# Two transformer blocks on one core: feed-forward input products from quarters, and the transposes of normed rows moved one block later

## The chip, the cores and the metric

The program runs on one core of a Trainium2 chip. The metric is the device time of one execution in microseconds (us). TensorE (PE) does the matrix products into PSUM; VectorE (DVE), ScalarE (ACT) and GpSimd (POOL) do the rest; SyncE (SP) issues the transfers.

## The reference, cut to what matters

Two blocks of a network follow one another on rows of width 1024: 512 rows of x and 256 of a context, all in 32-bit floats. There are four feed-forward parts (FFN 1 to 4 here, in order of time), each

```python
def swiglu(h, w_in, w_out):                     # h: T x 1024, w_in: 1024 x 5632, w_out: 2816 x 1024
    gate, up = jnp.split(h @ w_in, 2, axis=-1)
    return (jax.nn.silu(gate) * up) @ w_out
```

FFN 1 and FFN 3 work on T = 768 rows, FFN 2 and FFN 4 on T = 512. Between them lie mixers (linear attention, windowed and differential attention, a state-space scan). Before each FFN a residual sum is normed and scaled by a modulation: `x = layer_norm(ALPHA * x + g * mix(...))`, then `x * (1 + sc) + sh`.

## The kernel before

Every wide product is made of three passes: both factors are split into a high part (a cast, on ScalarE, L57) and a low part (a subtraction, on VectorE, L58), and PE sums high*high, high*low and low*high. `Core.split` does it, for 128x1024 tiles of weights too (`weight`, tiles `raw`, `whi`, `wlo`; three buffers of `raw`, four each of `whi` and `wlo`).

`ffn` (L363) has two stages. The input stage runs over j = 0 to 21. For each j it loads 128 gate columns and 128 up columns of `w_in` (each 128 x 8 x 128), splits them, and `mm_a` (L82) multiplies 8 pieces of the inner dimension in three passes: 48 matmuls of 512 columns, and for T = 768 another 48 of 256. `leave` takes silu (L385, ACT) and the product (L386, DVE) and stores the tile to DRAM (`gd`). It also runs `nfill` pieces of other work (`run_fill`): the products with `w_ada` and `mod_w` of later modulations, done on DVE (L223) for one or two vectors. The first two j are led in by `lead`: pieces of 256 rows, so that PE can work on the rows that are normed first while the last rows are still under way.

The output stage (L410 on) runs over the two halves of the rows, and for each over the 22 j in 18 groups: it loads 128 rows of `w_out` and the piece of `gd`, splits both, and `mm_b` (L96, L106) adds to the PSUM tiles of the half's rows, 128 rows at a time. In the last group each 128 rows go through `end.tail`: gate, residual, norm, and `to_hT` (L257): eight PE transposes (L269), scale and shift (L277 ACT, L280 DVE), and the split into `hhi` and `hlo`, the factors of the next stage. `rows_out` (L343) does the same for a mixer's output product.

The Tile framework fixes the order of each engine's queue ahead of the run from readiness and a priority that follows the program's order; `high_priority` moves weight loads and splits 400 places forward. A queue, SP's too, runs in order: an instruction that waits holds up those behind it.

Of the kernel before, what the change touches and what calls it, by code (L numbers as in the profile page):

```python
# [16 lines left out]
P = 128  # L17
D = 1024
# [6 lines left out]
class Core:  # L25


    def __init__(self, ctx, tc):
# [12 lines left out]
        self.fill = []  # L41

# [214 lines left out]
    def to_hT(self, pool, src, t, h, sc=None, bi=None, act=2):  # L257
# [3 lines left out]
        nc = self.nc  # L261
        hhi, hlo = h
# [80 lines left out]
def rows_out(c, w, parts, j0, T, put, px=False, scale=None):  # L343

    ws = [c.wrows(w, (j0 + i) * P, scale=scale) for i in range(len(parts))]
    ops = [(gh, gl, wh[:, 0], wl[:, 0]) for (gh, gl), (wh, wl) in zip(parts, ws)]
    for t in range(T // P):
        if px and t % 3 == 2:
            ps = [c.ps("px"), c.ps("px")]
            c.mm_b(ops, t * P, [(ps[0], 0, 512), (ps[1], 512, 512)])  # L350
            put(t, ps)
        else:
            pb = c.big()
            c.mm_b(ops, t * P, [(pb[:, :512], 0, 512), (pb[:, 512:], 512, 512)])
            put(t, [pb])

# [6 lines left out]
def ffn(c, h, T, w_in, w_out, end, nfill=2, lead=(0, 256)):  # L363
# [5 lines left out]
    nx = 512  # L369
    gd = [c.dram.tile([P, T], F32, name=c.nm("gd")) for _ in range(NJ)]  # L370
    with c.tc.tile_pool(name=c.nm("ffn"), bufs=2) as pool:

        def enter(j):
            pb = c.big()
            pc = c.ps("px") if T > nx else None
            og, ou = [(pb[:, :512], 0, nx)], [(pb[:, 512:], 0, nx)]
            if pc is not None:
                og.append((pc[:, :256], nx, 256))
                ou.append((pc[:, 256:], nx, 256))
            return c.wcols(w_in, j * P), c.wcols(w_in, FFN_H + j * P), og, ou  # L380

        def leave(j, og, ou):
            g = pool.tile([P, T], F32, tag="g", name=c.nm("g"), bufs=3)
            for (pg, t0, n), (pu, _, _) in zip(og, ou):
                nc.scalar.activation(g[:, t0 : t0 + n], pg, AF.Silu)  # L385
                nc.vector.tensor_tensor(g[:, t0 : t0 + n], pu, g[:, t0 : t0 + n], ALU.mult)  # L386
            nc.sync.dma_start(gd[j], g)
            if j >= 2:
                c.run_fill(nfill)

        ahead = [enter(j) for j in range(2)]
        for t0 in lead:
            for wg, wu, og, ou in ahead:
                for w_, outs in ((wg, og), (wu, ou)):
                    o, o0, _ = outs[t0 // nx]
                    c.mm_a(w_, h, [(o[:, t0 - o0 : t0 - o0 + 256], t0, 256)])
        for j in range(NJ):
            if j < len(ahead):
                leave(j, *ahead[j][2:])
                continue  # L400
            wg, wu, og, ou = enter(j)
            c.mm_a(wg, h, og)
            c.mm_a(wu, h, ou)
            leave(j, og, ou)
        c.run_fill(999)
        end.gate()
        end.fold()

        half = T // (2 * P)
        for first in (0, half):  # L410
            ts = range(first, first + half)
            c0, n = first * P, half * P
            out = {}

            def load(j):
                wh, wl = c.wrows(w_out, j * P)
                with c.tc.high_priority(offset=WPRIO):
                    gr = pool.tile([P, n], F32, tag="gr", name=c.nm("gr"), bufs=3)
                    nc.sync.dma_start(gr, gd[j][:, c0 : c0 + n])
# [5 lines left out]
            def room(t):  # L425
                if t % 3 == 2:
                    return [c.ps("px"), c.ps("px")]
                return [c.big()]

            js = [range(EDGE)] + [[j] for j in range(EDGE, NJ - EDGE)] + [range(NJ - EDGE, NJ)]  # L430
            for grp in js:
                ops = [load(j) for j in grp]
                for t in ts:
                    if t not in out:
                        out[t] = room(t)
                    c.mm_b(ops, (t - first) * P, halves(out[t]), grp[0] == 0, grp[-1] == NJ - 1)
                    if grp[-1] == NJ - 1:
                        end.tail(t, out[t])
        end.finish()
# [354 lines left out]
class LnTail:  # L794
# [4 lines left out]
    def __init__(self, c, pool, I, l, i, y, gates, resid, sc, xd, keep, hT=None, after=None, out=None, scaled=False):  # L799
        self.c, self.pool, self.y, self.gates = c, pool, y, gates  # L800
        self.resid, self.sc, self.xd, self.keep, self.after, self.out = resid, sc, xd, keep, after, out
        self.T = hT
# [3 lines left out]
        self.rows = (I["ln_g"][l, i : i + 1], I["ln_b"][l, i : i + 1])  # L806

# [36 lines left out]
    def fold(self):  # L844
# [4 lines left out]
        self.h = c.hT(self.T) if self.T else None  # L849

    def tail(self, t, pb):
# [4 lines left out]
        if self.after is None:  # L856
            c.to_hT(self.pool, y, t, self.h, *self.sc["x" if t < 4 else "c"], act=3)
# [21 lines left out]
class AdaTail:  # L879


    def __init__(self, c, pool, y, gates, resid, sc, xd, hT=None, out=None, ahead=2):
        self.c, self.pool, self.y, self.gates = c, pool, y, gates
        self.resid, self.sc, self.xd, self.T, self.out, self.ahead = resid, sc, xd, hT, out, ahead
        self.begun = set()
        self.scale = None

    def gate(self):
        self.g = self.gates()
# [10 lines left out]
    def fold(self):  # L900
        self.sc = self.sc()
        self.h = self.c.hT(self.T) if self.T else None
# [36 lines left out]
def ada_pre(c, pool, x, t, h, sc):  # L939
# [7 lines left out]
    c.to_hT(pool, xr, t, h, *sc, act=3)  # L947


def main(c, I, out, stop=None):  # L950
# [101 lines left out]
    with tc.tile_pool(name="mix0", bufs=1) as mp:  # L1052
# [58 lines left out]
        with tc.tile_pool(name="p1", bufs=1) as pool:  # L1111
            m = [pool.tile([P, KT, 768], F32R, name=f"m1{i}") for i in range(2)]
            for i, x in enumerate((og, od)):
                for t in range(6):
# [3 lines left out]
                        ln_sc("00", 0, 0, "scf0", "shf0", "xc"), xd[0], "xc", 768, out=out if stop == "ln1" else None)  # L1118
# [9 lines left out]
    with tc.tile_pool(name="p2", bufs=1) as pool, tc.tile_pool(name="modp1", bufs=2) as mq:  # L1128
# [4 lines left out]
        y = acc(pool, 6)  # L1133
        ln = LnTail(c, pool, I, 0, 1, y, {v: f"gf0{v}" for v in "xc"}, xdt(0),
                    ln_sc("01", 0, 1, "scm1", "shm1", "xc"), xd[1], "xc" if stop else "x", 768,
                    out=out if stop == "ln2" else None)
        ffn(c, h, 768, I["ffn_w_in"][0], I["ffn_w_out"][0], ln, 3, (0, 256, 512))
# [8 lines left out]
    with tc.tile_pool(name="p3", bufs=1) as pool:  # L1146
# [3 lines left out]
                    scaled=True)  # L1150
# [797 lines left out]
```

## Time and profile before

| what | value |
|---|---|
| median of 3 runs | 3626.3 us (3624.19 to 3632.98) |
| profiled execution, its own time | 3623.33 us |
| its span, first to last instruction | 3621.6 us |
| PE busy | 3479.2 us (96%) |
| DVE busy | 2134.4 us (59%) |
| ACT busy | 1503.7 us (42%) |
| POOL busy | 377.6 us (10%) |
| mean granted TensorE clock | 0.984 |

An engine is busy while one of its instructions runs; matmuls overlap, so a full PE bar means that PE had no idle time, not that it was at its peak. A row of a table of stretches gives the stretch, its length, for PE, PE's weight loads (PEld), DVE, ACT and POOL the busy us and the count of instructions, then the granted clock, the busy share of the DMA engines and GB/s. A row of a timeline gives start, duration, engine, line, operation, tiles, shapes and count; what stands in brackets is the idle time before it and what ended it. A row of waits gives total us, times, longest. A row of instructions of one line gives shortest/median/longest ns.

### The profile page before, as it was taken

The page shows a single profiled execution, that of the slowest core. Times are in us where ns is not written, and L with a number is a line of the kernel's source. Part 1 is how long each engine was busy: PE and PEld are TensorE (multiplying, and loading weights), DVE is VectorE, ACT ScalarE, POOL GpSimd, SP SyncE. Part 2 cuts the span into 40 slices and gives each one's busy share as a digit, 9 for nine tenths or more (in the row PEclk, how much of TensorE's full clock was granted, in tenths as well). Part 3 has the DMA queues.
Part 4 walks back from the last instruction along what each step waited for, and adds up shares of the span by engine and source line. Part 5 has one row for each costly group of instructions (what it writes and reads, how often), then busy time and mean ns, then how long its engine had stood idle before and what let it go on. Part 6 is the DMA issues. An engine that isn't in the chain of part 4 may idle for free. (4 is left out here: it accounts for less than half of the span.)

```text
span 3621.6 us, 48878 instructions
## 1 busy us (share of the span) xinstructions
PE 3479.2 (96%) x18988; PEld 2899.5 (80%) x18988; DVE 2134.4 (59%) x3246; ACT 1503.7 (42%) x2400; POOL 377.6 (10%) x309
## 2 busy tenths in 40 slices
PE   8999989999999999988999999999999999999999
PEld 5877778888878877767877788888887798878887
DVE  7766566554366577766566764443556585663245
ACT  5335533221344455533324632222556464553234
POOL 0001121000010354443000100000000000000000
PEclk9999999999999999989999999999999999999999
DMA  6331125555453233344665754654641112354456
GB/s 231 108 88 30 45 99 178 163 184 169 144 195 107 76 108 99 105 158 159 219 200 181 244 194 132 200 160 140 203 140 46 49 61 73 108 180 151 122 166 218
DMA packets 442652, 509.94 MB, mean 141 GB/s; under 512 B 20808, under 2 KB 355780, under 8 KB 442421
## 3 DMA queue, kind: packets, MB, share of 16 engines
q1 hardware_dynamic: 442421, 506.83, 44.3%
q8 instruction: 149, 2.44, 0.3%
q14 instruction: 82, 0.67, 0.1%
HBM read 446.20 MB, written 56.35 MB: 139 GB/s over the span
## 5 line engine op out<-in xcount | busy, mean ns | idle before, releaser
L58 DVE TENSOR_TENSOR wlo<-raw,whi 128x1024 fp32r<-128x1024 f32 (+1 forms) x524 | 639.9, 1225 | 661.8 <-ACT whi L57 632.9
L57 ACT CAST whi<-raw 128x1024 fp32r<-128x1024 f32 (+1 forms) x524 | 542.4, 1037 | 976.3 <-PE px L92 264.3
L92 PE MATMUL big<-hhi,whi 128*128 128x512 f32 (+1 forms) x2080 | 736.5, 370 | 9.8 <-ACT hhi L57 5.4
L92 PE MATMUL big<-hlo,whi 128*128 128x512 f32 (+1 forms) x2080 | 728.8, 367 | 3.6 <-DVE hlo L58 3.6
L92 PE MATMUL big<-hhi,wlo 128*128 128x512 f32 (+1 forms) x2080 | 731.1, 367 | 0.0
L92 PEld LDWEIGHTS big<-hhi,whi 128*128 128x128 f32 x2080 | 383.5, 191 | 85.3 <-issue 8.3
L92 PEld LDWEIGHTS big<-hlo,whi 128*128 128x128 f32 x2080 | 382.3, 191 | 69.8 <-DVE hlo L58 5.2
L92 PEld LDWEIGHTS big<-hhi,wlo 128*128 128x128 f32 x2080 | 382.3, 191 | 65.5 <-issue 1.9
L126 POOL TENSOR_TENSOR s<-s,mhalf 128x1 f32<-128x1 f32 (+1 forms) x106 | 72.8, 688 | 2656.8 <-DVE s L124 2350.3
L92 PE MATMUL px<-hhi,whi 128*128 128x256 f32 (+1 forms) x992 | 310.2, 316 | 3.6 <-ACT dqk L667 1.6
L92 PE MATMUL px<-hlo,whi 128*128 128x256 f32 (+1 forms) x992 | 309.0, 315 | 0.0
L92 PE MATMUL px<-hhi,wlo 128*128 128x256 f32 (+1 forms) x992 | 308.2, 314 | 0.0
L223 DVE SCALAR_TENSOR_TENSOR acc<-graw,silu_c,acc 128x1024 f32<-128x1024 f32 x168 | 211.7, 1292 | 78.0 <-DMA graw<-in_w_ada_dram 42.2
L106 PE MATMUL px<-whi,hhi 128*128 128x256 f32 (+1 forms) x712 | 213.2, 302 | 0.9 <-DVE wqf L620 0.7
L106 PE MATMUL px<-wlo,hhi 128*128 128x256 f32 (+1 forms) x712 | 211.4, 300 | 0.0
L106 PE MATMUL px<-whi,hlo 128*128 128x256 f32 (+1 forms) x712 | 211.1, 300 | 0.0
L92 PEld LDWEIGHTS px<-hhi,whi 128*128 128x128 f32 x992 | 186.3, 189 | 17.0 <-issue 2.1
L92 PEld LDWEIGHTS px<-hlo,whi 128*128 128x128 f32 x992 | 186.3, 189 | 10.7 <-issue 1.7
L92 PEld LDWEIGHTS px<-hhi,wlo 128*128 128x128 f32 x992 | 186.4, 189 | 10.2 <-issue 1.5
L57 ACT CAST ghi<-gr 128x256 fp32r<-128x256 f32 (+1 forms) x176 | 80.8, 460 | 273.8 <-PE px L106 159.0
L106 PE MATMUL big<-whi,ghi 128*128 128x512 f32 x616 | 191.4, 392 | 0.0
L106 PE MATMUL big<-whi,glo 128*128 128x512 f32 x616 | 191.4, 391 | 0.0
(545 smaller groups left out, 5976.8 us busy)
## 6 DMA issues: line engine op xcount, KB each, us to landing
raw<-in_ffn_w_in_dram SPq DMA_DIRECT2D x176, 512.0 KB
raw<-in_ffn_w_out_dram SPq DMA_DIRECT2D x176, 512.0 KB
graw<-in_mod_w_dram SPq DMA_DIRECT2D x80, 512.0 KB
graw<-in_w_ada_dram SPq DMA_DIRECT2D x72, 512.0 KB
raw<-in_mix_w_in_dram SPq DMA_DIRECT2D x42, 512.0 KB
raw<-in_ssd_w_in_dram SPq DMA_DIRECT2D x41, 512.0 KB
gd<-g SPq DMA_DIRECT2D x44, 384.0 KB
gr<-gd SPq DMA_DIRECT2D x88, 192.0 KB
```

The lines of the kernel that those rows point to most:

```text
L57: self.nc.scalar.copy(hi, src)
L58: self.nc.vector.tensor_tensor(lo, src, hi.bitcast(F32), ALU.subtract)
L92: self.nc.tensor.matmul(out, lhsT=w_[:, k, :], rhs=x_[:, k, t0 : t0 + tn], start=st, stop=sp)
L106: self.nc.tensor.matmul(out, lhsT=h_[:, t0 : t0 + P], rhs=w_[:, n0 : n0 + nn], start=st, stop=sp)
L126: nc.gpsimd.tensor_tensor(out=r, in0=v, in1=self.mhalf[:, :n], op=ALU.pow)
L223: nc.vector.scalar_tensor_tensor(a, raw, v[:, k : k + 1], a, ALU.mult, ALU.add)
```

## The change

The input stage takes a 2x2 partition of each j's product: the weights' blocks are (gate, up) x (inner half 1, 2), the rows' blocks are (inner half 1, 2) x (row half 1, 2). Eight products of quarters become seven in the Strassen-Winograd form, each of four pieces, three passes and n = T/2 columns: 84 matmuls of 384 columns (T = 768) or 256 (T = 512). Four sums of weight blocks per j are made on POOL, four sums of row blocks once per FFN on DVE and POOL (`Quarters.sums`). For these each normed 128 rows are stored to DRAM (`fd`) and read back. Intermediate products stay in PSUM and are copied out where a second result needs them. The weights come through four buffers of their own (`sr`) instead of `raw`. The fill runs 2 or 1 pieces per j and the rest in the output stage, one per group. The output stage has its own pool, opened after the input stage's pool closes, with the rows `y` in it.

`to_hT` of a normed tile is not issued at once but put in `c.later`; `flush` issues it behind the matmuls of the next 128 rows, and that of the last tile at the end.

```diff
+    def flush(self):
+        todo, self.later = self.later, []
+        for f in todo:
+            f()
...
     def to_hT(self, pool, src, t, h, sc=None, bi=None, act=2):
+        if isinstance(h, Quarters):
+            f = pool.tile([P, KT, P], F32, tag="hTf", name=self.nm("hTf"), bufs=h.bufs)
...
+            h.put(t, f)
+            return
...
 def rows_out(c, w, parts, j0, T, put, px=False, scale=None):
...
             c.mm_b(ops, t * P, [(pb[:, :512], 0, 512), (pb[:, 512:], 512, 512)])
+            c.flush()
             put(t, [pb])
+    c.flush()
...
+class Quarters:
+    def __init__(self, c, T, bufs=2):
+        self.c, self.n, self.half, self.bufs = c, T // 2, T // (2 * P), bufs
+        self.hi, self.lo = (x.rearrange("p k t -> p (k t)").rearrange("p (b k n) -> p b k n", b=4, k=4) for x in c.hT(T))
+        self.fd = [c.dram.tile([P, KT, P], F32, name=c.nm("fd")) for _ in range(T // P)]
+    def put(self, t, f):
+        c = self.c
+        c.nc.sync.dma_start(self.fd[t], f)
+        o = t % self.half * P
+        if t < self.half:
+            c.split(f.rearrange("p (b k) n -> p b k n", b=2), self.hi[:, 0:2, :, o : o + P], self.lo[:, 0:2, :, o : o + P])
+        else:
+            c.split(f[:, 4:], self.hi[:, 2, :, o : o + P], self.lo[:, 2, :, o : o + P])
+    def factors(self, pool):
+        c = self.c
+        self.t = [pool.tile([P, 3, 4, self.n], F32R, name=c.nm("tq")) for _ in range(2)]
+        q = lambda i: (self.hi[:, i], self.lo[:, i])
+        t = lambda i: (self.t[0][:, i], self.t[1][:, i])
+        return {1: q(0), 2: q(1), 3: q(2), 5: q(3), 6: t(0), 7: t(1), 4: t(2)}
+    def sums(self, pool, last):
+        c, nc = self.c, self.c.nc
+        for i in [i for i in range(self.half) if i != last] + [last]:
+            f1, f2 = (pool.tile([P, KT, P], F32, tag=f"f{j}", name=c.nm("f"), bufs=2) for j in range(2))
+            nc.sync.dma_start(f1, self.fd[i])
+            nc.sync.dma_start(f2, self.fd[i + self.half])
+            s = pool.tile([P, 4, 4, P], F32, tag="ts", name=c.nm("ts"), bufs=1)
+            nc.vector.tensor_tensor(s[:, 0], f2[:, :4], f1[:, :4], ALU.subtract)
+            nc.gpsimd.tensor_tensor(out=s[:, 2], in0=f2[:, 4:], in1=f2[:, :4], op=ALU.subtract)
+            nc.vector.tensor_tensor(s[:, 1], f2[:, 4:], s[:, 0], ALU.subtract)
+            nc.vector.tensor_tensor(s[:, 3], f1[:, 4:], s[:, 1], ALU.subtract)
+            o = slice(i * P, (i + 1) * P)
+            c.split(s[:, 0], self.hi[:, 3, :, o], self.lo[:, 3, :, o])
+            c.split(s[:, 1:], self.t[0][:, :, :, o], self.t[1][:, :, :, o])
...
+def ffn(c, h, T, w_in, w_out, end, nfill=(2, 1), last=None):
...
+    with c.tc.tile_pool(name=c.nm("fa"), bufs=1) as pool:
+        B = h.factors(pool)
+        def weights(j):
+            r = []
+            with c.tc.high_priority(offset=WPRIO):
+                for c0 in (j * P, FFN_H + j * P):
+                    x = pool.tile([P, KT, P], F32, tag="sr", name=c.nm("sr"), bufs=4)
+                    nc.sync.dma_start(x, w_in[:, c0 : c0 + P].rearrange("(k p) n -> p k n", p=P))
+                    r.append(x)
+                def pair(x):
+                    hi = c.whl.tile([P, KT, P], F32R, tag="hi", name=c.nm("whi"))
+                    lo = c.whl.tile([P, KT, P], F32R, tag="lo", name=c.nm("wlo"))
+                    c.split(x, hi, lo)
+                    return (hi[:, :4], lo[:, :4]), (hi[:, 4:], lo[:, 4:])
+                a11, a12 = pair(r[0])
+                a22 = tuple(pool.tile([P, 4, P], F32R, tag=f"a{i}", name=c.nm("a"), bufs=2) for i in range(2))
+                c.split(r[1][:, 4:], *a22)
+                p, q = r[0][:, :4], r[0][:, 4:]
+                u, v = r[1][:, :4], r[1][:, 4:]
+                for o, x, y, op in ((p, p, u, ALU.subtract), (u, u, v, ALU.add), (v, v, p, ALU.subtract),
+                                    (q, q, v, ALU.subtract)):
+                    nc.gpsimd.tensor_tensor(out=o, in0=x, in1=y, op=op)
+                s1, s2 = pair(r[1])
+                s3, s4 = pair(r[0])
+            return {1: a11, 2: a12, 3: s4, 4: a22, 5: s1, 6: s2, 7: s3}
+        def mul(out, j, i, start=False):
+            (wh, wl), (bh, bl) = W[j][i], B[i]
+            for k in range(4):
+                for w_, b_ in ((wh, bh), (wh, bl), (wl, bh)):
+                    nc.tensor.matmul(out, lhsT=w_[:, k], rhs=b_[:, k], start=start and k == 0 and w_ is wh and b_ is bh,
+                                     stop=k == 3 and w_ is wl, skip_group_check=True)
...
+        def first(j):
+            W[j] = weights(j)
+            X[j] = c.ps("px")[:, :n]
+            mul(X[j], j, 1, True)
+            S[j] = {1: room(pool, "p1")}
+            nc.scalar.copy(S[j][1], X[j])
+        def second(j):
...
+            Y[j], Z[j] = pb[:, :n], pb[:, 512 : 512 + n]
+            mul(Y[j], j, 2, True)
+            g = S[j][11] = room(pool, "c11")
+            nc.vector.tensor_tensor(g, Y[j], S[j][1], ALU.add)
+            nc.scalar.activation(g, g, AF.Silu)
+        for j in range(2):
+            first(j)
+            second(j)
+        with c.tc.tile_pool(name=c.nm("fs"), bufs=1) as fp:
+            h.sums(fp, half - 1 if last is None else last)
+        with c.tc.tile_pool(name=c.nm("fm"), bufs=1) as mp:
...
+            def third(j):
+                mul(Z[j], j, 3)
+                u, g = room(mp, "c12", 1), S[j]["g"]
+                nc.vector.tensor_tensor(u, Z[j], S[j][2], ALU.add)
+                nc.scalar.activation(u, u, AF.Silu)
+                nc.vector.tensor_tensor(g[:, n:], u, S[j][22], ALU.mult)
+                nc.sync.dma_start(gd[j], g)
+                c.run_fill(nfill[0])
+            for j in range(NJ + 1):
+                if j < NJ:
+                    sixth(j)
+                if j:
+                    fourth(j - 1)
+                if j < NJ:
+                    mul(Z[j], j, 5, True)
+                if j:
+                    third(j - 1)
+                if 0 < j < NJ - 1:
+                    first(j + 1)
+                if j < NJ:
+                    seventh(j)
+                if 0 < j < NJ - 1:
+                    second(j + 1)
+    with c.tc.tile_pool(name=c.nm("fb"), bufs=1) as pool:
+        end.open(pool)
...
+                if b == 0 and grp[-1] == NJ - 1:
+                    end.gate()
+                    end.fold()
...
+                    c.flush()
                     if grp[-1] == NJ - 1:
                         end.tail(t, out[t])
+                c.run_fill(nfill[1])
+        c.run_fill(999)
+        c.flush()
...
-    c.to_hT(pool, xr, t, h, *sc, act=3)
+    c.later.append(lambda: c.to_hT(pool, xr, t, h, *sc, act=3))
...
-        ffn(c, h, 768, I["ffn_w_in"][0], I["ffn_w_out"][0], ln, 3, (0, 256, 512))
+        ffn(c, h, 768, I["ffn_w_in"][0], I["ffn_w_out"][0], ln)
...
-        ffn(c, h, 512, I["ffn_w_in"][1], I["ffn_w_out"][1], ln)
+        ffn(c, h, 512, I["ffn_w_in"][1], I["ffn_w_out"][1], ln, (1, 1))
...
-        ffn(c, h, 768, I["ffn1_w_in_2"][0], I["ffn1_w_out_2"][0], ad, 3, (512, 0, 256))
+        ffn(c, h, 768, I["ffn1_w_in_2"][0], I["ffn1_w_out_2"][0], ad, last=0)
```

`sixth`, `fourth` and `seventh` multiply into `X` and hand it on in the same way: ACT copies of `X` (`u2`, `u3`), a DVE sum `c22` of `Z` and `u3`, and a DVE product of `X` with `c11` into `g`.

## Rows read from the trace of the kernel before

**Rows 1.** The page, busy time, share and instructions of each engine.
```profile
PE 3479.2 (96%) x18988; PEld 2899.5 (80%) x18988; DVE 2134.4 (59%) x3246; ACT 1503.7 (42%) x2400; POOL 377.6 (10%) x309
```
**Rows 2.** Stretches: FFN 3 and 4 input, 256-column product, FFN 2 output, FFN 4 start.
```profile
2150.00:2450.00 300.00, 300.00 (x1703) 258.29 (x1702) 142.77 (x152) 65.53 (x94) 0.00 (x0) 1.00 0.52 165
3300.00:3500.00 200.00, 200.00 (x885) 165.71 (x883) 56.69 (x58) 48.87 (x58) 0.00 (x0) 1.00 0.41 126
2955.00:2995.00 40.00, 40.00 (x331) 39.32 (x330) 34.15 (x67) 25.27 (x30) 0.00 (x0) 1.00 0.17 51
1984.00:2045.00 61.00, 61.00 (x271) 50.54 (x270) 44.17 (x59) 32.60 (x46) 0.55 (x1) 1.00 0.81 256
3252.00:3257.00 5.00, 5.00 (x35) 5.00 (x34) 3.21 (x6) 3.35 (x7) 0.72 (x2) 0.75 0.64 211
```
**Rows 3.** Groups of instructions (busy us, mean ns), then instructions of lines 58, 223, 386.
```profile
L57 ACT CAST whi<-raw 128x1024 fp32r<-128x1024 f32 x508 | 532.5, 1050 | 962.4 <-PE px L92 256.8 <-DMA raw<-in_ffn_w_in_dram 226.7 <-PE big L92 217.7
...
L58 DVE TENSOR_TENSOR wlo<-raw,whi x524: 681/1225/3267, 7.7 to 3603.5; 128x1024 fp32r<-128x1024 f32 x170, 128x512 fp32r<-128x512 f32 x5
L58 DVE TENSOR_TENSOR hlo<-hTf,hhi x64: 675/690/2883, 513.5 to 3264.2; 128x512 fp32r<-128x512 f32 x64
...
L223 DVE SCALAR_TENSOR_TENSOR acc<-graw,silu_c,acc x168: 1275/1280/3097, 573.4 to 2446.9; 128x1024 f32<-128x1024 f32 x168
...
L386 DVE TENSOR_TENSOR g<-big,g x88: 672/684/693, 569.0 to 3495.6; 128x512 f32<-128x512 f32 x88
L386 DVE TENSOR_TENSOR g<-px,g x44: 401/416/422, 584.8 to 2489.3; 128x256 f32<-128x256 f32 x44
```
**Rows 4.** POOL beside DVE: groups, line 1858, and the timelines near 556 us.
```profile
L58 DVE TENSOR_TENSOR hlo<-hTf,hhi 128x512 fp32r<-128x512 f32 x64 | 59.8, 947 | 13.8 <-ACT hhi L57 13.8
...
L1858 POOL TENSOR_TENSOR sbc<-sbc,sbias x32: 1037/1040/2022, 1191.7 to 1600.1; 128x512 f32<-128x512 f32 x32
...
556.10 2.36 POOL L873 TENSOR_TENSOR mix<-mix,lnb 128x1024 f32<-128x1024 f32 x1
...
556.30 2.71 DVE L58 TENSOR_TENSOR hlo<-hTf,hhi 128x512 fp32r<-128x512 f32 x1
```
**Rows 5.** PE's timeline: last output matmuls and last transposes before FFN 1 to 4.
```profile
543.68 0.61 PE L106 MATMUL px<-whi,m 128*128 128x512 f32 x2
...
559.39 0.66 PE L269 MATMUL mm<-cfs,mix 128*128 128x128 f32 x4 [1.02 <-DVE hTf L280]
...
1704.50 0.62 PE L106 MATMUL big<-whi,m 128*128 128x512 f32 x2
...
1720.32 1.10 PE L269 MATMUL mm<-cfs,y 128*128 128x128 f32 x8 [2.41 <-ACT y L767]
...
2099.58 0.62 PE L106 MATMUL big<-whi,glo 128*128 128x512 f32 x2
...
2125.76 1.09 PE L269 MATMUL mm<-cfs,xr 128*128 128x128 f32 x8 [2.26 <-ACT xr L946]
...
3243.75 0.61 PE L106 MATMUL big<-whi,mT 128*128 128x512 f32 x2
...
3259.46 1.03 PE L269 MATMUL mm<-cfs,xr 128*128 128x128 f32 x8
```
**Rows 6.** Waits of PE, longest in total first.
```profile
PE mm L269 <- ACT xr L946: 11.3, 11, 2.7
...
PE mm L269 <- ACT mix L767: 9.6, 6, 2.7
PE mm L269 <- ACT y L767: 8.8, 5, 2.6
```
**Rows 7.** SP's wait for a store, then a weight load's issue and its cast.
```profile
SPq L419 <- DMA gd<-g: 67.8, 23, 4.0
...
1797.66 0.38 SPq L67 DMA_DIRECT2D raw<-in_ffn_w_in_dram  x1
...
1802.76 1.05 ACT L57 CAST whi<-raw 128x1024 fp32r<-128x1024 f32 x1 [5.46 <-DMA raw<-in_ffn_w_in_dram]
```

More of the change, by code (lines that the diff above doesn't have):

```diff
@@ L261, in to_hT @@
         nc = self.nc
+        if isinstance(h, Quarters):
+            f = pool.tile([P, KT, P], F32, tag="hTf", name=self.nm("hTf"), bufs=h.bufs)
+            for half in range(2):
+                ps = self.ps()
+                for q in range(4):
+                    k = half * 4 + q
+                    nc.tensor.transpose(ps[:, q * P : (q + 1) * P], src[:, k * P : (k + 1) * P], self.ident)
+                for q in range(4):
+                    k = half * 4 + q
+                    if q < act:
+                        nc.scalar.activation(f[:, k, :], ps[:, q * P : (q + 1) * P], AF.Identity,
+                                             bias=bi[:, k : k + 1], scale=sc[:, k : k + 1])
+                    else:
+                        nc.vector.tensor_scalar(f[:, k, :], ps[:, q * P : (q + 1) * P], sc[:, k : k + 1],
+                                                bi[:, k : k + 1], ALU.mult, ALU.add)
+            h.put(t, f)
+            return
         hhi, hlo = h
@@ L368, in ffn @@
+def ffn(c, h, T, w_in, w_out, end, nfill=(2, 1), last=None):
     nc = c.nc
-    nx = 512
+    n, half = h.n, h.half
     gd = [c.dram.tile([P, T], F32, name=c.nm("gd")) for _ in range(NJ)]
-    with c.tc.tile_pool(name=c.nm("ffn"), bufs=2) as pool:
-        def enter(j):
-            pb = c.big()
[L375 to L412, printed above, removed]
@@ L413, in ffn @@
+    with c.tc.tile_pool(name=c.nm("fb"), bufs=1) as pool:
+        end.open(pool)
+        for b in (0, half):
+            ts = range(b, b + half)
             out = {}
@@ L806, in __init__, with open @@
         self.rows = (I["ln_g"][l, i : i + 1], I["ln_b"][l, i : i + 1])
+    def open(self, pool):
+        self.pool = pool
+        self.y = [pool.tile([P, D], F32, name=self.c.nm("y")) for _ in range(self.y)]
     def add_resid(self, t):
@@ L848, in fold @@
         self.sc = self.sc()
[L849 removed]
+        self.h = Quarters(c, self.T) if self.fast else c.hT(self.T)
     def tail(self, t, pb):
@@ L856, in tail @@
         if self.after is None:
-            c.to_hT(self.pool, y, t, self.h, *self.sc["x" if t < 4 else "c"], act=3)
+            c.later.append(lambda: c.to_hT(self.pool, y, t, self.h, *self.sc["x" if t < 4 else "c"], act=3))
         else:
@@ L901, in fold @@
         self.sc = self.sc()
-        self.h = self.c.hT(self.T) if self.T else None
+        self.h = None
+        if self.T:
+            self.h = Quarters(self.c, self.T, self.ahead) if self.fast else self.c.hT(self.T)
     def tail(self, t, pieces):
@@ L1126, in main @@
                 return
-    with tc.tile_pool(name="p2", bufs=1) as pool, tc.tile_pool(name="modp1", bufs=2) as mq:
+    with tc.tile_pool(name="modp1", bufs=2) as mq:
         modp[0] = accs(mq)
@@ L1191, in main @@
             return
-    with tc.tile_pool(name="p5", bufs=1) as pool, tc.tile_pool(name="modp3", bufs=2) as mq:
+    with tc.tile_pool(name="modp3", bufs=2) as mq:
         modp[0] = accs(mq)
```

77 lines of the change are left out of this document (46 added, 31 removed).

## Prediction

> **What bounds the kernel now.** I read the page's busy times first: PE is busy 96% of the span [rows 1], so time is to be had from PE's own work and from what little idle time it has. Then the stretches, to see what PE pays per matmul. In FFN 4's input stage PE has no idle moment and issues 885 matmuls of 512 columns in 200 us, 226.0 ns each; in a stretch of a mixer 331 of 256 columns in 40 us, 120.8 ns; in FFN 3's input stage, where the two sizes alternate, 1703 in 300 us, 176.2 ns on the mean, against 173.4 for the midpoint of the other two [rows 2]. So twice the columns cost 1.87 times the time: about 15 ns of a matmul are there whatever its width. Fewer columns are worth something, smaller matmuls cost something. Then the groups by line for what DVE, ACT and POOL pay per tile [rows 3, 4], the timeline of PE at the four entries into an FFN [rows 5], PE's waits [rows 6] and the transfers [rows 7].
>
> **Matmuls of the input stages.** T = 768: before, 96 matmuls per j at 176.2 ns, 16.91 us; after, 84 of 384 columns at an estimated 173.4 ns, 14.57 us (at most 176.2, 14.80 us). 2.35 us by 44 j are 103 us (at least 93). T = 512: before, 48 at 226.0 ns, 10.85 us; after, 84 at 120.8, 10.15 us; 0.70 by 44 are 31 us. So an eighth of the columns goes in both, yet at T = 512 half of the worth goes back because the matmuls halve. The lead of 256-row pieces goes too: 288 matmuls at 120.8 ns are 34.8 us where two j cost 33.8, and 192 are 23.2 where they cost 21.7: 2 x 1.0 + 2 x 1.5 = 5 us [rows 2]. Gain: 139 us (129 to 139).
>
> **What the other engines must do in that time.** Per j, after: DVE splits three weight tiles of 128x1024 (1.225 us each) and one of 128x512 (0.69), and takes five results of n columns: 0.55 each at 384 (between 0.416 and 0.684) [rows 3]. That is 7.1 us at T = 768 and 6.45 at T = 512 (five by 0.416). A fill piece with two vectors adds 2 x 1.28 = 2.56, one with a single vector 1.28. FFN 1 has 30 of either kind and runs 44 in the stage, two per j: 12.2 us in its first 15 j, 9.7 later, of 14.57. FFN 3 has 20 of the double kind: ten j of 12.2. FFN 2 runs one per j, ten single and twelve double: 7.7, then 9.0, of 10.15. FFN 4 has none. POOL makes four sums of 128x512: line 1858 has 1.04 us for one, so 4.2 us per j [rows 4].
>
> DVE alone would fit. But the two engines get in each other's way: beside a POOL addition from 556.10 to 558.46 a DVE subtraction of 128x512 took 2.71 us, where the median is 0.69, and the mean of these 64 is 947 ns [rows 3, 4]. It ended 0.55 us after POOL did, as if it had waited for it. Per j then DVE loses between nothing and 4.2 us. The 64 subtractions lost 64 x 0.257 = 16 us, in a phase where POOL was only sometimes at work, so I take 0.4 of POOL's time: 1.7 us. DVE then has 13.9 of 14.57 at worst at T = 768, and 9.4, then 10.7, of 10.15 in FFN 2. What isn't hidden: 12 x 0.5 = 6 us in FFN 2, and for waits on DVE where it is over 90% full (25 j at T = 768 and 22 of FFN 2) some 0.4 us each, 19 us. Taken: 25 us. If POOL never blocks, nothing; if it always does, DVE needs 16.4 in 25 j (1.8 over PE), 11.9 and 13.2 in FFN 2 (1.7 over in ten, 3.0 in twelve), 10.6 in FFN 4 (0.5 over in 22): 45 + 17 + 36 + 11 = 109 us.
>
> The Trainium skill, page SBUF — State Buffer, section Who interferes with whom, speaks against the change: a DVE instruction with both inputs in SBUF and a GpSimd instruction that reads SBUF share a read interface as an exclusive lock, and the later one waits for the whole of the other. The 2.71 us row agrees. By that rule every weight split (raw minus whi) contends with the four new sums, and the loss would lie nearer to 109 than to 25.
>
> **The entry into each FFN.** Here a wait is added. Before, `lead` gives PE pieces of the first normed rows while the last are under way, and PE loses about 4 us per entry (the brackets show 1.0 to 2.4 for the last tile). After, PE has only products 1 and 2 of two j until `sums` is done: 48 matmuls, 8.3 us at T = 768, 5.8 at T = 512. The rest waits for the last tile, by a chain that the trace lets me add up. From the end of the last output matmul to the end of the last transposes: 560.05 - 544.29 = 15.8, 1721.42 - 1705.12 = 16.3, 2126.85 - 2100.20 = 26.7, 3260.49 - 3244.36 = 16.1 us [rows 5]. Then scale and shift of the tile's second half, 2.0 us (between one and four passes of 0.69) [rows 3]; its store, 3.5 us (SP, when it got there, still waited 67.8/23 = 2.9 us on the mean for a `gd` store to land, at most 4.0); its load, 4.0 us (a 512 KB load took 5.1 from issue to cast beside others) [rows 7]; three DVE sums of 128x512, 2.1, the cast and the subtraction of 128x1536, 1.6 and 1.8 [rows 3]: 15.0 us. Product 6 starts 30.8, 31.3, 41.7 and 31.1 us after the output matmuls; PE's work in it is 8.3 or 5.8 and 2.2 of transposes; idle are 20 + 23 + 31 + 23 = 97, less 16 before: 81. The first part may be shorter, because `lead`'s own splits and results no longer stand in DVE's queue: I take 75 us. If it shrinks by 8 us each and a transfer takes 2.9, 40 us; if the weights' new buffers `sr`, in memory that the stage before still uses, come later than the chain, 100. Behind the weights' loads stand the stores `fd` in SP's queue, and whoever needs a weight waits with them; PE has nothing else to do then anyway. In 3252 to 3257, behind the entry into FFN 4, the granted clock was 0.75, between the two levels of 1.2 and 2.4 GHz, and 35 matmuls were issued where 41 fit [rows 2]; after longer idle times I take 2 us per entry, 8 us (4 to 14).
>
> **Input to output stage.** The pool `fb` lies where `fa` lay, so the first `gr` loads can wait for product 4 of the last j to let go of the row sums: 4.0 for the load and 1.0 for its split, less product 3 (2.1 or 1.4 us): 3 us by four, 12 us (0 to 14).
>
> **Fill in the output stage.** Of FFN 2's 40 pieces 18 are left, 14 of them with a load of 512 KB. The stage's DMA is at 0.81 and 256 GB/s without them [rows 2], so 316 at full; 7.3 MB take 23 us if nothing else yields. They can spread over both halves, 119 us with a fifth free, so nothing at best. Taken: 8 us. FFN 1 and 3 have 4.06 us per j there, where 2.7 is FFN 2's, and hide theirs.
>
> **Transposes behind the next matmuls.** PE waited 11.3 + 9.6 + 8.8 = 29.7 us for the normed rows before a transpose [rows 6]. With a block of matmuls between, such a wait goes, but not at a stage's last tile. Taken: 20 us (0 to 30).
>
> **Sum.** 139 + 20 - 25 - 75 - 8 - 12 - 8 = 31 us. From the profiled execution's 3623.3 that is 3592; the median of the runs lies 3.0 higher, so 3595.
>
> **Rivals.**
> A. POOL's sums always hold up DVE's splits, and DVE sets the pace: 109 lost where I have 25, 3679 us. For it: the 2.71 us row. Against: it needs DVE to have a two-input subtraction at the head of its queue each time; four of the five results of a j come from PSUM. It decides from a loss of 56 us on (25 + 31): there the change stops being faster. Chance 0.20; this one ends slower.
> B. The entries cost little, 30 us where I have 75, since DVE is freer: 3550 us. For it: a subtraction that should take 0.69 took 2.71 in that very chain. Against: store and load must follow one another. Chance 0.17.
> C. The entries cost 106 us: the gain is spent, 3626 us, no change to be seen. For it: nothing but four products covers a chain of 31 us or more. Against: 15 of the 16 us before the transposes are mostly queueing. Chance 0.17.
> D. The weight buffers: three of four per j are held; if the first pair of j + 1 gets the one that product 3 of j - 1 frees just before product 1 of j + 1, PE waits for a cast and a split, 1.05 + 1.23 = 2.3 us [rows 3], 80 times: 182 us, 3777. Against: product 2 frees a buffer five products before. Chance 0.06.
> The forecast, 3575 to 3614 or so: 0.40.
>
> **Numbers.** A measurement of this kernel tells 0.3%, 11 us, from no change. Faster: the forecast and B, less what of the forecast lies within 11 us: 0.55. Same: C and that edge: 0.18. Slower: A, D: 0.27. The range goes down to 3540 (B with 10 us to spare) and up to 3680 (A); the forecast's own is 3575 to 3614.
>
> **What would show it.** Right: in the input stages 84 matmuls per j at about 173 and 121 ns, PE near full, periods of 14.6 to 15 and 10.2 to 10.7 us; four idle stretches of 15 to 30 us ahead of product 6, ended by DVE's low part of the row sums; transposes without waits except at the last tile. Wrong: DVE over 95% in the input stages and PE waiting for `wlo` all along (A); idle under 10 us at an entry (B); waits for `whi` at each product 1 (D).

## The result: 3922 us, 8% slower

The changed kernel takes 3922.1 us in the median against 3629.6 us for the kernel before beside it: ratio 1.080, 95% interval 1.077 to 1.083. The prediction was 3595 us, at most 3680. One of experiment 12's four runs took 4253 us at a granted clock of 0.737, and its time below is the median of the other three.

The profiled execution spans 3917.0 us, 295.4 more than before, at a granted clock of 0.943 (0.984). Its busy row, to be read beside [rows 1]:

```profile
PE 3446.8 (88%) x19660; PEld 2986.7 (76%) x19660; DVE 2535.7 (65%) x3760; ACT 1775.9 (45%) x2883; POOL 925.1 (24%) x671
```

PE is idle for 3917.0 - 3446.8 = 470 us, where it was 142: 328 more. Its busy time is only 32 us less, though the products alone should have saved 139; the rest, some 107 us, by subtraction went on matmuls at the lower clock level behind idle times. No engine is full. PE's waits, longest in total first, beside [rows 6]:

```profile
PE big L479 <- DVE c L529: 75.9, 40, 4.1
PE px L479 <- ACT whi L64: 55.9, 8, 16.5
PE big L479 <- ACT hhi L64: 45.7, 3, 16.5
PE mm L275 <- ACT xr L1102: 43.5, 7, 17.8
PE big L113 <- ACT ghi L64: 32.9, 3, 11.8
```

Three places are named: the steps (L529 adds u2 to product 3 and so frees its accumulator), the entries (`whi`, `hhi`, `xr`), and the change from input to output products (`ghi`).

**The steps.** Stretches of the changed kernel: FFN 1's steps, then FFN 4's, where no fill runs (beside the first two of [rows 2]).

```profile
650.00:950.00 300.00, 280.36 (x1543) 271.05 (x1542) 208.64 (x228) 122.29 (x183) 115.48 (x71) 0.97 0.41 130
...
3500.00:3750.00 250.00, 213.59 (x1613) 209.37 (x1612) 130.49 (x169) 102.70 (x171) 101.33 (x76) 0.93 0.32 95
```

In FFN 4 DVE is busy 52% of the time, ACT and POOL 41%, PE 85%: this is no bound by one engine's work. A step there, median distance between two stores of `g`, takes 12.66 us where 84 matmuls need 10.1 and the kernel before took 10.88. One step in order of time, picked from the engines' timelines:

```profile
3698.27 0.58 PE L479 MATMUL big<-hhi,whi 128*128 128x256 f32 x1 [2.18 <-DVE c L529]
...
3699.08 0.41 PE L479 MATMUL big<-hhi,whi 128*128 128x256 f32 x1
3699.29 0.41 PE L479 MATMUL big<-hlo,whi 128*128 128x256 f32 x1
...
3701.07 1.05 ACT L64 CAST whi<-sr 128x1024 fp32r<-128x1024 f32 x1 [2.08 <-issue]
...
3702.15 1.23 DVE L65 TENSOR_TENSOR wlo<-sr,whi 128x1024 fp32r<-128x1024 f32 x1 [0.49 <-ACT whi L64]
...
3703.45 1.29 POOL L470 TENSOR_TENSOR sr<-sr,sr 128x512 f32<-128x512 f32 x1 [7.91 <-DVE wlo L65]
...
3704.83 1.29 POOL L470 TENSOR_TENSOR sr<-sr 128x512 f32<-128x512 f32 x1
...
3704.89 1.78 DVE L65 TENSOR_TENSOR a<-sr,a 128x512 fp32r<-128x512 f32 x1
...
3706.81 2.67 POOL L470 TENSOR_TENSOR sr<-sr,sr 128x512 f32<-128x512 f32 x2 [0.69 <-DVE a L65]
...
3709.21 2.62 DVE L65 TENSOR_TENSOR wlo<-sr,whi 128x1024 fp32r<-128x1024 f32 x2 [2.54 <-ACT whi L64]
...
3711.74 0.42 DVE L529 TENSOR_TENSOR c<-big,u 128x256 f32<-128x256 f32 x1
...
3712.21 0.39 PE L479 MATMUL big<-hhi,whi 128*128 128x256 f32 x1 [2.14 <-DVE c L529]
```

Product 2 of one step ends near 3701 and lets go of a weight buffer; the cast of a later step's first pair starts. (The cast's row names no releaser. That it waits for this buffer is inferred from the times, here and one step on, and from experiment 4.) Its split, POOL's sums in place, the next casts and two splits follow one another; behind those in DVE's queue stands L529, and behind L529 waits the next product 2. From 3701.07 to 3712.21 that is 11.1 us, with product 2 itself 13 to 14: a chain that goes round once per step, while each engine rests. The first three rows show product 2 behind such a wait of 2.18 us: 0.21 us apart, where full clock gives 0.12 [rows 2]. The small split of `a` started 0.06 us after a POOL sum and took 1.78 us, and POOL's last two sums waited for it.

At T = 768 the chain shows less. The median step there is 14.6 us, which is what its matmuls need, but steps of 17 to 24 us come between (mean 15.9 in FFN 1).

**The entries.** The kernel before, then the changed one, at FFN 1 to 4:

```profile
500.00:632.00 132.00, 120.55 (x736) 106.23 (x735) 88.91 (x115) 47.89 (x81) 32.90 (x18) 0.99 0.43 143
1690.00:1800.00 110.00, 101.35 (x531) 87.09 (x530) 64.97 (x79) 46.03 (x70) 23.21 (x13) 0.97 0.59 189
2045.00:2170.00 125.00, 117.17 (x694) 103.21 (x693) 90.19 (x112) 61.15 (x96) 11.88 (x9) 0.99 0.65 208
3230.00:3300.00 70.00, 65.15 (x377) 57.65 (x376) 38.24 (x52) 40.56 (x68) 3.84 (x7) 0.95 0.58 181
```
```profile
500.00:632.00 132.00, 80.03 (x369) 68.93 (x368) 102.46 (x122) 50.54 (x80) 58.03 (x33) 0.81 0.46 156
1690.00:1806.00 116.00, 79.45 (x400) 67.81 (x399) 80.87 (x91) 44.00 (x68) 56.08 (x30) 0.81 0.55 188
2190.00:2350.00 160.00, 98.28 (x431) 83.54 (x430) 113.55 (x135) 71.38 (x107) 37.52 (x25) 0.79 0.56 187
3440.00:3517.00 77.00, 44.51 (x250) 39.48 (x249) 43.20 (x55) 41.84 (x71) 23.62 (x20) 0.73 0.45 147
```

Idle (length less PE) was 11.5 + 8.7 + 7.8 + 4.9 = 33 us and is 52.0 + 36.6 + 61.7 + 32.5 = 183: 150 more. In the changed kernel's four stretches PE waits 68 us ahead of transposes, 56 for the first weights (`whi`) and 46 for the row sums (`hhi`).

**The exits**: four idle stretches of 11.8, 10.9, 11.3 and 10.2 us, the first of which shows as

```profile
965.10 0.33 SPq L532 DMA_DIRECT2D gd<-g  x1
...
970.17 1.28 SPq L561 DMA_DIRECT2D gr<-gd  x3
...
974.24 1.19 PE L113 MATMUL big<-whi,ghi 128*128 128x512 f32 x2 [11.80 <-ACT ghi L64]
```

The load of `gr` is issued 5 us after the last store of `g`, and SP's last wait ahead of it is for that store to land (2.4 us).

**FFN 2's output stage** takes 170.2 us where it took 130.9.

### The profile page after: what moved, and what is told of

Read it like the earlier page. It is cut to its first block, busy times and chain, and to the rows that moved or that the text cites. A ratio compares the mean times of both kernels' runs of the same rounds, so it can differ in the third digit from the quotient of the medians.

```text
span 3917.0 us, 52389 instructions
## 1 busy us (share of the span) xinstructions
PE 3446.8 (88%) x19660; PEld 2986.7 (76%) x19660; DVE 2535.7 (65%) x3760; ACT 1775.9 (45%) x2883; POOL 925.1 (24%) x671
## 4 chain that ended last, share of the span: by engine, by line
PE 35%; DVE 11%; POOL 9%; DMA 5%; ACT 5%; issue 4%; SPq 0%; POOLq 0%; DVEq 0%; ACTq 0%
PE big L113 8%; PE px L113 7%; POOL sr L470 6%; PE px L479 5%; PE big L479 4%; PE px L99 4%; DVE wlo L65 3%; ACT whi L64 3%; PE big L99 2%; DVE sxT L1895 1%; DVE acc L230 1%; PE mm L1536 1%; DMA raw<-in_ffn_w_out_dram 1%; PE mm L1709 1%; POOL syg L2031 1%
## 5 line engine op out<-in xcount | busy, mean ns | idle before, releaser
L470 POOL TENSOR_TENSOR sr<-sr,sr 128x512 f32<-128x512 f32 x264 | 390.4, 1479 | 768.1 <-DVE wlo L65 700.3
L65 DVE TENSOR_TENSOR wlo<-raw,whi 128x1024 fp32r<-128x1024 f32 (+1 forms) x348 | 421.3, 1216 | 230.3 <-ACT whi L64 218.0
L65 DVE TENSOR_TENSOR wlo<-sr,whi 128x1024 fp32r<-128x1024 f32 x264 | 345.7, 1311 | 262.1 <-ACT whi L64 260.0
L64 ACT CAST whi<-sr 128x1024 fp32r<-128x1024 f32 x264 | 276.9, 1050 | 475.4 <-POOL sr L470 347.7
L479 PE MATMUL big<-hhi,whi 128*128 128x256 f32 (+1 forms) x1056 | 346.7, 329 | 121.6 <-DVE c L529 75.9
L479 PE MATMUL px<-tq,whi 128*128 128x384 f32 (+1 forms) x1408 | 331.4, 323 | 30.6 <-ACT p L493 28.3
L479 PE MATMUL big<-hlo,whi 128*128 128x256 f32 (+1 forms) x1056 | 341.5, 323 | 2.2 <-DVE hlo L65 2.2
L479 PE MATMUL big<-hhi,wlo 128*128 128x256 f32 (+1 forms) x1056 | 340.9, 323 | 0.0
L479 PEld LDWEIGHTS px<-tq,whi 128*128 128x128 f32 x1408 | 252.7, 203 | 37.2 <-ACT p L493 32.5
L479 PE MATMUL px<-tq,wlo 128*128 128x256 f32 (+1 forms) x704 | 224.5, 319 | 0.3 <-DVE wlo L65 0.3
```

Of the source, the lines that this page charges most:

```text
L64: self.nc.scalar.copy(hi, src)
L65: self.nc.vector.tensor_tensor(lo, src, hi.bitcast(F32), ALU.subtract)
L470: nc.gpsimd.tensor_tensor(out=o, in0=x, in1=y, op=op)
L479: nc.tensor.matmul(out, lhsT=w_[:, k], rhs=b_[:, k], start=start and k == 0 and w_ is wh and b_ is bh, stop=k == 3 and w_ is wl, skip_grou ...
```

## The experiments

Those marked "change +" start from the changed kernel; their times stand beside 3922. Experiments 1, 12 and 16 have three or more runs, the others one each. Runs of one kernel differ by 10 us (changed) to 22 us (before), so a few us in a single run tell nothing. Steps are medians over a stage.

**1. Deferred transposes alone, on the kernel before** (`later` and `flush`, nothing else).

> The deferred transposes alone, on the kernel before, with its old input stage. My prediction's term says 20 us less than the kernel before (0 to 30), so about 3605. The rival, that the PE waits at the transposes only move to another place or that the deferral delays the normed rows that the next stage starts on, says 0 to 20 us more, so 3630 to 3650.

3626.5 us, ratio 0.9993 (0.9978 to 1.0008). The term of 20 us is nothing. The waits before transposes are what they were (11.1 + 9.5 + 8.3 us), and the two traces show why: of PE's 18,988 matmuls, transposes among them, all but 187 stand in the same place of its order. Wherever the program issues the transposes, the framework, which orders the queues by readiness, puts them in nearly the same place.

**2. Change + L529 one place forward in DVE's queue.**

```diff
-                nc.vector.tensor_tensor(u, Z[j], S[j][2], ALU.add)
+                with c.tc.high_priority(offset=2 * WPRIO):
+                    nc.vector.tensor_tensor(u, Z[j], S[j][2], ALU.add)
```

> The changed kernel with one edit: the DVE addition that reads product 3's accumulator (Z + u2) stands ahead of the last weight split in DVE's queue, no longer behind it. Theory 'queue': the gap of 2.18 us ahead of product 2 in each T=512 step is DVE's two splits of 1.3 us standing ahead of that addition; one less ahead takes 1.3 us from each of some 40 steps, and a little clock with it: 50 to 70 us less than the changed kernel, about 3855. Theory 'loop through the weight buffers': the same work goes round, the wait moves to the weights; within 15 us of the changed kernel, about 3910.

3871.9 us, 50 less. FFN 4's step fell from 12.66 to 11.27, 1.4 us: about the one split of 1.3 that no longer stands on the way, though the small split fell too, from 1.11 to 0.73 us on the mean. The order in the queue is part of the loop.

**3. Change + no sums of weight blocks** (the `gpsimd.tensor_tensor` loop of `weights` deleted).

> The changed kernel without GpSimd's four sums of weight blocks (the splits then take unsummed blocks, so this leaves part of the computation out). Theory 'loop': the sums are 4 x 1.3 us and the blocked split 1.1 us of a chain of some 13 us that goes round once in each step; without them a T=512 step falls from 12.5 to 13.9 us to TensorE's own 10.2 to 10.6, a T=768 step from 16.6 to about 14.7: 42 x 2.5 + 42 x 1.8 is 180 us less than the changed kernel, about 3740. Theory 'entries and exits are all of it': GpSimd is off the path, and 20 us or less is gained, about 3900.

3730.1 us, 192 less. Steps of 10.08 (T = 512) and 14.55 us (T = 768). POOL's sums are on the path; but without them the kernel is still 100 us slower than before.

**4. Change + two weight buffers of its own for the first pair at T = 512** (`a11, a12 = pair(r[0], own)`, tiles in `fa`).

> The changed kernel with two weight buffers of its own for the pair that product 1 and 2 read, at T=512 alone; the four shared buffers are left to the two other pairs. Theory 'loop': the cast of that pair no longer waits until product 2 of the step before has ended, the chain starts up to a step earlier, and a T=512 step falls to 10.5 to 11.5 us: 42 x 2 is about 85 us less than the changed kernel, 3830. Theory 'queue' alone: both splits still stand ahead of the addition, the gap of 2.18 us stays, and the time stays within 15 us of the changed kernel.

3955.6 us, 33 more, where the theories said 85 less or no change: both numbers were missed. FFN 4's step is 13.9. SP's, ACT's and POOL's timelines in it:

```profile
3641.20 1.58 SPq L454 DMA_DIRECT2D sr<-in_ffn_w_in_dram  x2
...
3645.12 1.05 ACT L64 CAST whi<-sr 128x1024 fp32r<-128x1024 f32 x1 [1.62 <-DMA sr<-in_ffn_w_in_dram]
...
3647.27 0.62 ACT L64 CAST a<-sr 128x512 fp32r<-128x512 f32 x1 [0.52 <-PE px L479]
...
3661.24 1.29 POOL L470 TENSOR_TENSOR sr<-sr,sr 128x512 f32<-128x512 f32 x1 [7.71 <-DMA sr<-in_ffn_w_in_dram]
```

The freed cast now stands a step ahead in ACT's queue, where it waits for its load, issued only 3.9 us before. The load waits for a staging tile `sr` that the last split of an earlier step frees. The casts behind it wait too. The loop closed through the next scarce buffer.

**5. Change + the sums on DVE** (`nc.vector.tensor_tensor(o, x, y, op)` in place of the POOL form).

> The changed kernel with the four sums of weight blocks on DVE instead of GpSimd, all else as it was; in DVE's queue the addition that frees product 3's accumulator then stands ahead of both splits. Theory 'loop': the chain of one T=512 step loses 4 x (1.3 - 0.7) us and the blocked split's 1.1 us, and no DVE operation is stretched; DVE's own work is about 9.3 us a step, under TensorE's 10.1. Steps of 10.2 to 11.3 at T=512 (12.7 before the edit) and fewer long steps at T=768: 80 to 120 us less than the changed kernel, 3800 to 3840. Theory 'DVE is the bound': the steps become 13 us and more, 3920 or above.

3743.3 us, 179 less: nearly all that leaving the sums out gave. FFN 4's and FFN 1's steps in it:

```profile
3420.00:3590.00 170.00, 170.00 (x1419) 170.00 (x1418) 147.64 (x220) 89.28 (x153) 0.00 (x0) 1.00 0.41 123
640.00:930.00 290.00, 289.06 (x1650) 282.72 (x1649) 239.64 (x314) 131.20 (x195) 0.00 (x0) 1.00 0.46 143
```

In FFN 4 PE has no idle moment, 1419 matmuls in 170 us are 119.8 ns each, the clock is full, and DVE carries 87%. DVE's groups in this stretch, then DVE's and POOL's in the changed kernel's FFN 4:

```profile
L65 DVE TENSOR_TENSOR wlo<-sr,whi 128x1024 fp32r<-128x1024 f32 x51 | 61.0, 1223 | 12.1 <-ACT whi L64 9.8
L470 DVE TENSOR_TENSOR sr<-sr,sr 128x512 f32<-128x512 f32 x51 | 35.1, 689 | 1.2
...
L65 DVE TENSOR_TENSOR a<-sr,a 128x512 fp32r<-128x512 f32 x17 | 11.6, 684 | 0.0
```
```profile
L65 DVE TENSOR_TENSOR wlo<-sr,whi 128x1024 fp32r<-128x1024 f32 x57 | 72.1, 1265 | 70.9 <-ACT whi L64 70.3
L65 DVE TENSOR_TENSOR a<-sr,a 128x512 fp32r<-128x512 f32 x19 | 21.1, 1111 | 2.0
...
L470 POOL TENSOR_TENSOR sr<-sr,sr 128x512 f32<-128x512 f32 x57 | 73.8, 1295 | 147.7 <-DVE wlo L65 137.7 <-DVE a L65 7.8
L470 POOL TENSOR_TENSOR sr<-sr 128x512 f32<-128x512 f32 x19 | 27.5, 1448 | 1.5
```

A sum is 0.69 us on DVE and 1.3 to 1.45 on POOL; beside POOL the small split takes 1.11 us on the mean, alone 0.68. By the mean step of each stage, about 115 of the 179 us are won at T = 512 and 50 at T = 768.

**6. Change + the tiles of g in a pool ahead of `fa`** (`gr` at both sizes, `ghi` and `glo` at T = 512).

> The changed kernel with the tiles that the output stage reads g into in a pool of their own, opened ahead of the input stage's pool (the raw tiles at both sizes, the split tiles at T=512 too). Theory 'the first g loads wait for the input stage's memory': the four idle stretches of 10.2 to 11.8 us at the change from input to output products fall to some 3 us, 30 to 35 us less than the changed kernel, about 3888. Rival, that they wait for the last product's g to reach DRAM and come back: the stretches stay at 10 us or more, within 12 us of the changed kernel.

3878.4 us, 44 less. At T = 512 the idle stretches are gone; at T = 768, where only `gr` found room, they are 8.8 and 8.2 us. (The waits that went add up to 27 us; the rest of the 44 has not been followed up.)

**7. Change + no row sums, nor their way through DRAM** (products 4 to 7 take plain quarters).

> The changed kernel without the sums of row quarters and their way through DRAM; products 4 to 7 take plain quarters, so this leaves part of the computation out. Theory 'entries': the 12.8 to 16.5 us ahead of product 6 in each of the four stages go (58 us), with some half-clock matmuls behind them: 55 to 75 us less than the changed kernel, about 3855. Rival, that the late first weights (16.5, 13.4, 9.9 and 6.0 us ahead of product 1) hold the entry by themselves and what stands behind them only moves: 20 us less or none.

3849.9 us, 72 less, as the theory said (55 to 75).

**8. Change + both buffers (4), a fifth `sr`, and the order (2), at T = 512.**

> At T=512 alone, product 1's and 2's weights in buffers of their own, a fifth staging tile for the raw weights, and the freeing addition ahead of the last split as in the second experiment. Theory 'loop': with buffers alone (3956 us) the same chain closed through the staging tiles, a cast that waits for its load standing ahead of the other casts on ScalarE; with a fifth tile that load no longer waits, and the T=512 step falls to TensorE's 10.2 to 10.6 us: 42 x 2.4 is 100 us less than the changed kernel, about 3820. Rival, that it is GpSimd's lock on DVE and not the buffers: the step stays at 11.3 us or more, 3870 or above.

3873.5 us, 49 less; the step is 11.09. The time is the rival's, the step lies between the two theories': the loop got shorter than in 2 and 4, yet POOL's 5.5 us of sums stay in it. The small split is hardly held up any more (0.75 us on the mean). In most steps PE still waits 0.76 us for the sum of L529.

**9. Change + FFN 2's fill as in the other stages** (`(2, 1)` for `(1, 1)`).

> The changed kernel with one argument changed: in the second feed-forward two fill steps follow each input step and one each output step, no longer one and one. Theory 'the fill in the output stage costs': its output stage falls from 170 us towards the 131 us of the kernel before, and the norm chain behind it, in which ten and more DVE fill operations of 1.24 us stand, is shorter by 10 to 18 us; the input steps of that stage get 10 to 20 us longer. 25 to 45 us less than the changed kernel, about 3885. Rival, that the fill costs as much wherever it stands: within 12 us of the changed kernel.

3901.9 us, 20 less, between the theory's 25 to 45 and the rival's 12. The output stage fell to 132.2, the stretch before it grew from 918 to 934 us. The entry into FFN 3 did not get shorter: its wait of 18 us for `xr` has another cause.

**10. Change + the first step's raw weights in tiles that outlive the stage.**

> The changed kernel with the raw weights of the first step of each input stage in staging tiles that outlive the stages, so that they can be loaded while the mixer's output products still run. Theory 'late first weights': the waits of 16.5, 13.4, 9.9 and 4.4 us for the first weights fall to some 2.5 us, 30 us less than the changed kernel, about 3890. Rival, that the row sums end the entry and product 6 waits for them as before: the waits for weights shrink, those for the row sums grow by as much, within 12 us of the changed kernel.

3911.3 us, 11 less: the rival. PE's waits for `whi` fell from 55.9 to 44.3 us in all, those for the row sums (`hhi`) grew from 45.7 to 61.8: the weights were late, but the row sums end the entry.

**11. The edits 5, 6 and 9 together.**

> Three of the edits together: weight sums on DVE (179 us less alone), the output stage's g tiles opened early (44 less alone), the second feed-forward's fill back in its input stage (35 by the theory above). If they add up, 3922 - 179 - 44 - 35 is 3664. If the fill on DVE and the sums on DVE get in each other's way in the T=512 steps, 3690 to 3710.

3707.0 us, 28 above the sum of the three gains as measured (43 above the one expected, which put the fill at 35). FFN 2's steps, with the fill and the weight sums both on DVE, have two of 23.9 and 25.3 us.

**12. The same and the order of the entry's queues** (edit 10; `high_priority` around the row sums; product 6's sum split first).

> The same three edits, and the entry: the first weights in the staging tiles that outlive the stages, and the row sums, their loads and splits ahead of the fill's DVE operations and of the second step's weight loads in the queues, the sum that product 6 reads split first. Theory 'the entry is a queue order': some 10 DVE operations of 1.24 us and 5 us of load issues no longer stand ahead of the row sums, 12 to 20 us in each of four entries: 50 to 80 us less than the run before, 3585 to 3615, faster than the kernel before. Rival, that the way of the last row block through DRAM and the splits set the entry: 20 us less or none, 3640 or above.

3692.3 us, ratio 1.017 (1.015 to 1.019), 15 less than experiment 11: again the rival. Entry into FFN 1, from the engines' and SP's timelines:

```profile
563.50 1.42 DVE L65 TENSOR_TENSOR hlo<-hTf,hhi 128x512 fp32r<-128x512 f32 x1 [0.69 <-ACT hhi L64]
...
564.45 2.67 POOL L1030 TENSOR_TENSOR mix<-mix,lnb 128x1024 f32<-128x1024 f32 x1
...
567.15 0.32 SPq L1031 DMA_DIRECT2D xd<-mix  x1
567.56 0.38 SPq L403 DMA_DIRECT2D fd<-hTf  x1
...
572.02 0.79 SPq L424 DMA_DIRECT2D f<-fd  x2
...
579.51 1.86 POOL L428 TENSOR_TENSOR ts<-f 128x512 f32<-128x512 f32 x1 [12.38 <-DMA f<-fd]
580.16 1.75 DVE L427 TENSOR_TENSOR ts<-f,f 128x512 f32<-128x512 f32 x1
...
584.93 1.04 ACT L64 CAST whi<-sr 128x1024 fp32r<-128x1024 f32 x1
...
586.03 0.69 PE L484 MATMUL px<-hhi,whi 128*128 128x384 f32 x1 [25.66 <-ACT whi L64]
```

The last store of rows stands in SP's queue behind one that waits for POOL, and from that store to the first sum (POOL's, which waits for the load) the round trip takes 12 us. PE's longest wait here, 25.7 us, ends with a weight cast: in ACT's queue it now stands behind casts of the row sums.

**13. Twelve without row sums.**

> The last kernel above (sums on DVE, early g tiles, fill, entry order) without the row sums and their way through DRAM; products 4 to 7 take plain quarters, so this leaves part of the computation out. Theory 'the entries are what is left': 3692 falls by 70 us or more, to 3620 or less, at or under the kernel before. Rival, that the norm chain of the last row blocks, which nothing covers any more, is what is left and the row sums only stand behind it: 3650 or above.

3617.2 us, 75 less, and 16 under the 3633.5 of the kernel before beside it, in a single run: without the row sums and their way through DRAM, 12 would be at or under the kernel before.

**14 and 15. Twelve with the row stores in ACT's queue; with the `xd` stores in POOL's.**

> The same kernel with the stores of the transposed rows to DRAM issued by ScalarE's queue in place of SyncE's, where they stood behind the stores of normed rows that wait for GpSimd (4 to 5.5 us late for the last row block at the first entry). Theory 'queue order': 4 to 5 us at the entries behind a LayerNorm, less behind the others: 8 to 20 us less than 3692. Rival, that the round trip through DRAM (some 12 us from store to the first sum) and not its start sets it: within 8 us.

> The same kernel with the stores of the normed rows issued by GpSimd's own queue, so that SyncE's is free of that wait for every load and store behind it, the row loads and the second step's weights too. Theory 'queue order': 8 to 25 us less than 3692. Rival as above: within 8 us.

3686.6 and 3690.8 us, 6 and 2 less, which single runs do not tell from nothing: the queue's order is little. How the 75 us of experiment 13 divide between the round trip and the sums themselves, no run shows.

**16. Seven products at T = 768 alone.** FFN 2 and 4 as in the kernel before, with `lead`; FFN 1 and 3 with the edits of 12 and 14, one buffer in place of two for the second row tile of the sums, and

```diff
+                    two = b == 0 and j < 2
+                    gh, gl = ((gp if two else pool).tile([P, n], F32R, ...) for t in ("ghi", "glo"))
...
-            js = [range(EDGE)] + [[j] for j in range(EDGE, NJ - EDGE)] + ...
+            js = [range(2)] + [[j] for j in range(2, NJ - EDGE)] + ...
```

> Seven products at T=768 alone, with the edits so far and the first two steps' g tiles ahead of the input stage; the T=512 stages are those of the kernel before with their lead over rows. By the stages measured, T=512 cost 32 + 4 + 9 + 3 us more than in the kernel before: 3692 - 48 is 3644; the change from input to output products gives 8 us at each of two stages, with half-clock matmuls behind them: 3620 to 3632, the kernel before within 0.3%. If the entry's order of queues is worth as much as theory 'queue order' says, 3610. Rival, that steps and exits give less at T=768 than their stretches show: 3645 or above.

3609.5 us, ratio 0.994 (0.992 to 0.996): 0.6% under the kernel before. From the end of one output stage to the start of the next, FFN 1 to 4: 920.5, 840.4, 373.6 and 819.1 us, before 932.4, 846.5, 386.3 and 822.5. No idle time is left at the exits; the T = 768 output stages are 10 and 8 us longer, with 32 and 31 more matmuls in them. In each, some 26 are the input stage's last products, which now run behind the first output products, and 8 are the fill's, of which one piece per j runs there.

## Why the prediction was wrong

**Matmuls (139): right.** With the sums on DVE a step takes 10.08 and 14.56 us; 44 x (17.00 - 14.56) + 44 x (10.88 - 10.08) = 143, with 17.00 and 10.88 the steps of the kernel before.

**DVE and POOL (25, at most 109): the step that failed.** It cost 179 us (experiment 5). The prediction added up each engine's work per j, found DVE's within PE's time, and stopped at "DVE alone would fit". It did fit: DVE is 52% busy in FFN 4. What was never added up is one step's chain from engine to engine, and the four weight buffers and DVE's queue that close it into a loop. POOL's four sums, put at 4.2 us per j, took 5.3. Rival A had the right parts and the wrong mechanism (DVE full); rival D looked at the buffers, but priced one cast and one split at 2.3 us. The lock that the Trainium skill describes (SBUF — State Buffer, Who interferes with whom) shows: 1.11 us against 0.68 for the split beside POOL. Priced as DVE's capacity it explains nothing here, as a link of the loop something. How the 179 us divide between POOL's slower sums, the lock and the place of L529 is not settled; the edit of the place alone gives 50 (experiment 2), and it takes most of the lock's cost with it.

**Entries (75, at most 106): too small.** PE's idle time there is 150 us more. Leaving out the row sums gave 72 to 75 us (experiments 7, 13); the prediction named their chain, but put store and load at 7.5 us where 12 pass in experiment 12. That its 75 comes near those gains is chance: it was to cover the whole entry. Missed was the rest, the waits ahead of transposes (17.8 us ahead of FFN 3's alone) and for weights. The likeliest reason: PE had `lead`'s products of rows already normed under the 16 us of the norm chain, and now has products 1 and 2, which wait for whole halves of the rows and for weights. No experiment tests that.

**Exits (12): 44.** The waits were foreseen at 3 us each by load and split of one piece; they were 10 to 12. That they wait for memory was right (experiments 6 and 16), but at the first exit SP's rows end the wait with the last store of `g`, not with product 4.

**FFN 2's fill (8): 39 in the output stage**, 20 net of what it costs in the input stage. **Transposes (20): 2**, not told from nothing. **Clock (8):** PE's busy time fell by 32 where 143 were saved, so about 110 us went on slower matmuls; this is not a term of its own but the echo of every short wait, and goes when the waits go (granted clock 1.00 in both stretches of experiment 5).

The gain of 143 less 179, 150, 44 and 20 makes 250 us slower, where 292 were measured. The parts overlap and were not all measured in the same way; what the other 40 us are is open. Part of it is likely to be the slower matmuls of the entries (granted clock 0.73 to 0.81), which an idle time does not count.

## What to carry to other kernels

Before trusting that extra work "fits" beside a full engine, add up one step's chain through all engines, with its position in each in-order queue, and count the buffers that close it: a loop of 13 us through half-idle engines beat every capacity sum. Here a buffer added to the loop moved it to the next scarce buffer (33 us more), and shortening the chain is what helped. Where a rearrangement takes away work that covered a latency, price the latency in full. In these runs the seven products won only when they were used at T = 768 alone, where a step saves 2.4 us; with T = 512, where it saves 0.8, they did not (T = 512 alone was not run).

## What the runs showed of the hardware

Behind a wait of 2.2 us once per step the matmuls ran, in some of the steps, at the lower clock level (0.21 us apart for 256 columns, as behind 3698.27 us, and not 0.12); behind the next one, 2.14 us at 3712.21, they ran 0.12 apart. The granted clock of FFN 4's steps was 0.93. A DVE sum of 128x512 from SBUF takes 0.69 us where POOL needs 1.3 to 1.45, so the idle engine was the wrong one for work on the path.
